# The next chunk's projection moved into the middle of a top-k chunk, ahead of its last two blocks, with one dot per top-k step

## The chip, the cores and the metric

The kernel runs on one core of one Trainium2 chip. The metric is the device time of one execution in microseconds. A core has a matrix engine (TensorE, PE in the profile, with its weight loads PEld), a vector engine (VectorE, DVE), a scalar engine (ScalarE, ACT), GpSimd (POOL), and SyncE (SP), which here only issues DMAs. Each engine works through its own queue in order and waits on semaphores for the others.

## The reference

Two layers over 512 tokens of width 1024. Each has a mixer (pooling and retention in layer 0, a gated recurrence in layer 1) and then PEER, a channel mixer that picks experts by product keys. The change touches PEER only, and it is the same in both layers:

```python
q = (xt @ w_q).reshape(T, PEER_HEADS, 2, PEER_HALF)
s = jnp.einsum('thpd,hpkd->thpk', q, sub_keys)
s_top, i_top = lax.top_k(s, PEER_TOPK)
cand = s_top[:, :, 0, :, None] + s_top[:, :, 1, None, :]
best, pos = lax.top_k(cand, PEER_TOPK)
eid = ...
gate = jax.nn.softmax(best, axis=-1)
act = jax.nn.gelu(jnp.einsum('td,thkd->thk', xt, u_sel))
return jnp.einsum('thk,thkd->td', gate * act, v_sel)
```

There are 8 heads with two halves each, 128 keys per half, the best 16 of each, and 16 experts of 16384 per token and head.

## The kernel before, in words

Weights come from DRAM by `stream` (L172): SP loads 512 KB into one of five `raw` buffers, ScalarE casts it to a rounded part `hi` (L169), and VectorE takes the rest as `lo` (L170). There are six `hi`/`lo` buffers. TensorE then multiplies in three passes (`mm3`, L185 to L187). A buffer is free again when TensorE has used it.

Most of PEER is done densely. For all 16384 experts the activation of tokens 32 to 383 is computed in 128 blocks of 128 experts (`mm1`, 24 matmuls of 352 columns each); the result is multiplied with a gate array that holds zeros nearly everywhere, and multiplied with the v table (`mm2`, L1098). 84 of the 128 blocks (`lookahead`, L756) can be done before the gates are known: they are the work that fills TensorE while VectorE does the routing. They are called lookahead blocks below.

`route_topk` (L767) does the routing in four chunks of two heads (four half-heads). In each chunk TensorE makes the q projection (`proj_T`, 4 x 24 matmuls of 512 columns; ScalarE copies each of the four heads to `qh`, L781), then for each of four token blocks (tb 0 to 3, 128 tokens each) four score matmuls (L851). VectorE finds the top 16 of each half-head in five steps (L860 to L864; one such group is called a head below), twenty steps per token block.

Token block 0 is finished chunk by chunk: `choose` picks the experts of two heads, and `Scatter.place` (L78) computes their addresses. The first 32 tokens of block 0 are not done densely: for them GpSimd fetches the u rows of their experts by indirect DMA (`urow`, L741, eight fetches of 128 rows per chunk, into seven buffers), VectorE takes eight dots per chunk (L105), and `weigh` (L107) puts a Gelu of the dots on ScalarE (`actu`, L111) and multiplies it into the gates (L113). Then `Scatter.add` (L116) adds the gates of block 0 into the DRAM array `gz`, sixteen indirect DMAs per head on GpSimd (L127). Each head's adds wait for those of the head before. On GpSimd's queue stand: chunk 0's rows, the adds of head 0, chunk 1's rows, the adds of head 1, chunk 2's rows, the adds of head 2, chunk 3's rows, and all other adds.

After the chunks, token blocks 3, 1 and 2 get their `choose` for all eight heads, `route_gates` (L885) builds the gate array (VectorE makes one-hot tiles, TensorE multiplies them, L912 and L913, ScalarE scales, SP stores to `gd`, L918), and `experts` (L998) reads `gd` and `gz` back and runs the expert matmuls.

How much lookahead stands between the routing steps is set by credits that the generators yield:

```python
for cost in gen:
    credit += cost
    while credit >= 2.8:
        credit -= 2.8
        next(look, None)
```

A yield of 2.8 thus emits one lookahead block. The order of instructions within an engine is then set by a scheduler that follows the emitted order with its own estimate of times; `tc.issue_after` holds an instruction behind another one.

Before the change, a chunk emits: projection; for each token block its scores, its four heads, and a yield of 1.5 to 4 (`YC`, by chunk); after block 0 `choose`, and after blocks 2 and 3 four dots each. The four weight tiles of the next projection are streamed ahead of the last four dots.

Of the kernel before, what the change touches and what calls it, by code (L numbers as in the profile page):

```python
# [9 lines left out]
F32 = mybir.dt.float32  # L10
F32R = mybir.dt.float32r
F16 = mybir.dt.float16
U32 = mybir.dt.uint32
# [7 lines left out]
P = 128  # L21
T = 512
NTB = T // P
D = 1024
# [12 lines left out]
QC = 32 // QN  # L37
# [7 lines left out]
RAW = 5  # L45
QS = 8
Y2 = 1.6
YC = (1.5, 3.0, 3.0, 4.0)
AHEAD = 4
TAIL = 4  # L50
CREDIT0 = 0.0
# [2 lines left out]
NEG = -3.0e38  # L54
# [88 lines left out]
class Kern:  # L143
# [589 lines left out]
        return xT  # L733

    def urow(self, pool, layer, ids, j):
        if self.urows % 7 == 6:
            t = self.pe.tile([P, D], F32, name="urow3", tag="lnb")
        else:
            t = pool.tile([P, D], F32, name="urow", tag="urow", bufs=6)
        self.urows += 1  # L740
        d = self.nc.gpsimd.indirect_dma_start(out=t, out_offset=None, in_=self.io["u%d" % layer],  # L741
                                              in_offset=bass.IndirectOffsetOnAxis(ap=ids[:, j:j + 1], axis=0))
        return t, d.ins
# [23 lines left out]
    def route_topk(self, layer, xT, kT, gz):  # L767
        nc, tc, io = self.nc, self.tc, self.io
        with tc.tile_pool(name="rt", bufs=1) as rt, tc.tile_pool(name="rt2", bufs=2) as rt2, \
# [5 lines left out]
            stop = rt.tile([P, NTB, 16, 16], F32, name="stop", tag="stop")  # L775
            itop = rt.tile([P, NTB, 16, 16], F16, name="itop", tag="itop")
            wq = io["peer_w_q"][layer]

            def sink_q(n, ps):
                q = rt2.tile([P, T], F32, name="qh", tag="qh", bufs=5)  # L780
                nc.scalar.copy(q, ps)  # L781
                qs.append(q)

# [55 lines left out]
                nc.scalar.copy(ghT, gs)  # L839
                nc.vector.tensor_tensor(glT, gs, ghT, ALU.subtract)  # L840

            for c in range(4):
                qs = []
                keys = rt2.tile([P, 4, P], F32, name="keys", tag="keys")
                nc.sync.dma_start(out=keys, in_=io["keysT"][layer][:, c * 4:c * 4 + 4, :])
                self.proj_T(wq, c, xT, sink_q, early=c == 0)
                for tb in range(NTB):
                    ts = slice(tb * P, (tb + 1) * P)
                    ps = self.psB.tile([P, 512], F32, name="pB", tag="pB")
                    for i in range(4):  # L850
                        nc.tensor.matmul(ps[:, i * P:(i + 1) * P], qs[i][:, ts], keys[:, i, :],  # L851
                                         start=True, stop=True)
                    ixs = rs2.tile([P, 4, 16], U32, name="ix", tag="ix", bufs=2)
                    for i in range(4):
                        hp = c * 4 + i
                        sc = ps[:, i * P:(i + 1) * P]
                        mx = stop[:, tb, hp, :]
                        ix = ixs[:, i, :]
                        s2 = rs2.tile([P, P], F32, name="s2", tag="s2")
                        nc.vector.max(out=mx[:, 0:8], in_=sc)  # L860
                        nc.vector.max_index(out=ix[:, 0:8], in_max=mx[:, 0:8], in_values=sc)
                        nc.vector.match_replace(out=s2, in_to_replace=mx[:, 0:8], in_values=sc, imm_value=NEG)
                        nc.vector.max(out=mx[:, 8:16], in_=s2)
                        top = nc.vector.max_index(out=ix[:, 8:16], in_max=mx[:, 8:16], in_values=s2)  # L864
                    nc.vector.tensor_copy(itop[:, tb, c * 4:c * 4 + 4, :], ixs)
                    yield YC[c]
                    if tb == 0:
                        yield from choose(0, c * 2, 2)
                        if c:
                            gz.add(self)  # L870
                    else:
                        n = (0, 1, 1)[tb - 1] * QC // 2
                        if tb == 3 and c < 3:
                            self.w0 = [self.stream(wq[c + 1, k]) for k in range(4)]
                        yield 1.3 * n
                        with tc.issue_after(top.ins):
                            gz.dots(self, n)
                gz.weigh(self, rs2)
                if c == 0:
                    gz.add(self)  # L880
# [350 lines left out]
```

## Time and profile before

| what | value |
|---|---|
| median of three runs | 2781.21 us (2779.95 to 2781.95) |
| the profiled execution | 2778.95 us |
| its span | 2777.2 us |
| TensorE busy | 2737.9 us (99%) |
| VectorE busy | 2357.1 us (85%) |
| first score of layer 0, of layer 1 | 188.9 us, 1624.2 us |
| last scores of layer 0, of layer 1 | 412.0 us, 1847.6 us |
| gate matmuls of layer 0 | 525.9 to 619.1 us |
| gate matmuls of layer 1 | to 2054.5 us |

Times in the profile count from the start of the span. "Busy" of VectorE is overstated a little in the top-k stages: one instruction's record overlaps the next one's by 0.1 us or so, and what counts is the distance from start to start. The same holds for TensorE, whose matmuls are pipelined: 24 matmuls with records of 0.32 us each take 24 times the step between their starts. A wait in square brackets is the idle time ahead of an instruction, with what ended it.

### The profile page before, as it was taken

To read this page: it belongs to the slowest core of one execution; us is meant where nothing else is said; L and a number is where in the kernel's file an instruction comes from. 1 tells how busy PE (TensorE), PEld (TensorE's weight loads), DVE (VectorE), ACT (ScalarE), POOL (GpSimd) and SP (SyncE) were. 2 spreads that over 40 slices of the span, in tenths; PEclk is the share of its full clock that TensorE was granted. 3 is DMA by queue.
4 is the path that set the end of the run, shared out by engine and by line. 5 is a ranking of instruction groups with operands and counts; after the bars stand their busy time and mean duration, and the time that the engine had idled before them with its cause. 6 is when DMAs were issued, how large, how long until landed. Compare 5 with 4: busy or idle time off the path is not lost.

```text
span 2777.2 us, 41653 instructions
## 1 busy us (share of the span) xinstructions
PE 2737.9 (99%) x15314; PEld 2442.7 (88%) x15314; DVE 2357.1 (85%) x4556; ACT 1115.8 (40%) x1575; POOL 1344.2 (48%) x865
## 2 busy tenths in 40 slices
PE   9999899999999999999999998999999999999998
PEld 7898899999888888888788898999998888888886
DVE  6678789886899989998798678789868999899988
ACT  3353335553333333333334343346553333333332
POOL 0006558774556555653000017558754566566652
PEclk9999999999999999999999999999999999999999
DMA  6357677899999999998222557667999999999994
GB/s 231 122 183 218 205 220 203 225 301 367 355 396 406 394 403 400 404 396 307 96 84 73 205 176 200 196 215 189 266 310 344 396 407 406 386 389 409 404 380 172
DMA packets 319470, 794.12 MB, mean 286 GB/s; under 512 B 62240, under 2 KB 128288, under 8 KB 319264
## 3 DMA queue, kind: packets, MB, share of 16 engines
q1 hardware_dynamic: 176384, 413.64, 42.1%
q0 software_dynamic: 120128, 303.22, 31.0%
q10 hardware_dynamic: 22752, 74.59, 6.7%
q8 instruction: 120, 1.97, 0.3%
q14 instruction: 86, 0.70, 0.1%
HBM read 711.38 MB, written 79.95 MB: 285 GB/s over the span
## 4 chain that ended last, share of the span: by engine, by line
PE 85%; issue 7%; DVE 3%; POOL 3%; DMA 2%; ACT 0%; SPq 0%; DVEq 0%; POOLq 0%; ACTq 0%
PE pC L1098 19%; PE pB L1098 19%; PE pA L187 11%; PE pA L185 11%; PE pA L186 11%; PE pC L185 3%; PE pC L187 3%; PE pC L186 3%; POOL gz L127 2%; DMA urow<-in_u,ids 1%; PE pB L912 1%; PE pB L913 1%; PE pB L851 1%; DVE oh L902 1%; POOL urow L741 1%
## 5 line engine op out<-in xcount | busy, mean ns | idle before, releaser
L169 ACT CAST hi<-raw 128x1024 fp32r<-128x1024 f32 (+1 forms) x609 | 636.3, 1050 | 920.3 <-PE pC L1098 216.0
L170 DVE TENSOR_TENSOR lo<-raw,hi 128x1024 fp32r<-128x1024 f32 (+1 forms) x609 | 730.3, 1215 | 188.6 <-ACT hi L169 183.2
L970 POOL DMA_INDIRECT row<-in_u,eid x256 | 402.6, 1573 | 441.7 <-DVE av L982 392.5
L185 PE MATMUL pA<-xThi,hi 128*128 128x352 f32 (+2 forms) x1808 | 606.7, 336 | 1.9 <-ACT hi L169 1.4
L187 PE MATMUL pA<-xThi,lo 128*128 128x352 f32 (+2 forms) x1808 | 604.3, 334 | 0.9 <-DVE lo L170 0.9
L186 PE MATMUL pA<-xTlo,hi 128*128 128x352 f32 (+2 forms) x1808 | 604.1, 334 | 0.8 <-DVE xTlo L170 0.8
L127 POOL DMA_INDIRECT gz<-gate,idx x256 | 494.2, 1930 | 132.4 <-issue 79.9
L970 POOL DMA_INDIRECT row<-in_v,eid x256 | 356.2, 1391 | 145.0 <-DVE h L995 66.8
L995 DVE SCALAR_TENSOR_TENSOR h<-row,cf,h 128x1024 f32<-128x1024 f32 x256 | 329.6, 1288 | 42.7 <-DMA row<-in_v,eid 42.0
L185 PEld LDWEIGHTS pA<-xThi,hi 128*128 128x128 f32 x1808 | 339.7, 188 | 19.2 <-ACT hi L169 2.5
L186 PEld LDWEIGHTS pA<-xTlo,hi 128*128 128x128 f32 x1808 | 339.6, 188 | 16.7 <-DVE xTlo L170 1.2
L187 PEld LDWEIGHTS pA<-xThi,lo 128*128 128x128 f32 x1808 | 339.5, 188 | 16.5 <-DVE lo L170 2.2
L982 DVE CUSTOM_DVE_ANT_0 row<-row,x 128x1024 f32<-128x1024 f32 x256 | 311.3, 1220 | 20.7 <-DMA row<-in_u,eid 20.4
L1098 PE MATMUL pC<-hi,ch 128*128 128x512 f32 x768 | 299.1, 389 | 0.0
L1098 PE MATMUL pB<-hi,cl 128*128 128x512 f32 x768 | 299.1, 389 | 0.0
L1098 PE MATMUL pB<-hi,ch 128*128 128x512 f32 x768 | 299.0, 389 | 0.0
L1098 PE MATMUL pC<-lo,ch 128*128 128x512 f32 x768 | 299.0, 389 | 0.0
L1098 PE MATMUL pC<-hi,cl 128*128 128x512 f32 x768 | 298.9, 389 | 0.0
L1098 PE MATMUL pB<-lo,ch 128*128 128x512 f32 x768 | 298.8, 389 | 0.0
L187 PE MATMUL pC<-xThi,lo 128*128 128x352 f32 x672 | 218.6, 325 | 17.4 <-DVE lo L170 17.3
L169 ACT CAST ch<-gt 128x768 fp32r<-128x768 f32 x128 | 107.1, 837 | 311.1 <-DVE gt L1061 216.8
L185 PE MATMUL pC<-xThi,hi 128*128 128x352 f32 x672 | 220.4, 328 | 0.1
(280 smaller groups left out, 4410.5 us busy)
## 6 DMA issues: line engine op xcount, KB each, us to landing
raw<-in_peer_ut SPq DMA_DIRECT2D x256, 512.0 KB, 6.6
raw<-in_peer_v SPq DMA_DIRECT2D x256, 512.0 KB, 7.6
gd<-gbuf SPq DMA_DIRECT2D x16, 2048.0 KB, 10.5
gt<-gd ACTq DMA_DIRECT2D x60, 512.0 KB, 7.6
sp<-ge SPq DMA_DIRECT2D x38, 704.0 KB, 5.1
ge<-sp ACTq DMA_DIRECT2D x38, 704.0 KB, 8.3
raw<-in_peer_w_q SPq DMA_DIRECT2D x32, 512.0 KB, 4.8
gz<-zero SPq DMA_DIRECT2D x64, 256.0 KB, 4.2
```

What stands on the lines that cost most here:

```text
L127: d = nc.gpsimd.indirect_dma_start(out=flat, out_offset=bass.IndirectOffsetOnAxis(ap=self.idx[c][:, j:j + 1], axis=0), in_=gate[:, j:j + 1 ...
L169: self.nc.scalar.copy(hi, src)
L170: return self.nc.vector.tensor_tensor(lo, src, hi.bitcast(F32), ALU.subtract)
L185: nc.tensor.matmul(ps, ah, bh, start=(first and i == 0), stop=False)
L186: nc.tensor.matmul(ps, ah, bl, start=False, stop=False)
L187: nc.tensor.matmul(ps, al, bh, start=False, stop=(last and i == n - 1))
L741: d = self.nc.gpsimd.indirect_dma_start(out=t, out_offset=None, in_=self.io["u%d" % layer], in_offset=bass.IndirectOffsetOnAxis(ap=ids[:, ...
L851: nc.tensor.matmul(ps[:, i * P:(i + 1) * P], qs[i][:, ts], keys[:, i, :], start=True, stop=True)
L970: nc.gpsimd.indirect_dma_start(out=t, out_offset=None, in_=io[name], in_offset=bass.IndirectOffsetOnAxis(ap=at, axis=0))
L982: dot = nc.vector.tensor_tensor_reduce(ur, ur, x, 1.0, 0.0, ALU.mult, ALU.add, av[:, k:k + 1])
L995: nc.vector.scalar_tensor_tensor(acc, vr, c, acc, ALU.mult, ALU.add)
L1098: nc.tensor.matmul(acc[hf], a[:, ts], b[:, hf * 512:(hf + 1) * 512], start=first and i == 0, stop=last and i == 2)
```

## The change

A chunk is now emitted in another order. The projection of chunk 0 comes first. Then, in each chunk: scores and heads of token block 0, with a yield of `YA` = 2.3 after each head; `choose`; scores and heads of block 1, each head with one of the four weight tiles of the next projection and a yield of 2.3; the scores of blocks 2 and 3 together; the whole next projection; and then the eight heads of blocks 2 and 3, each followed by one dot (held behind the head's last step) and a yield of `YB`, 0.2 in chunks 0 to 2 and 2.4 in chunk 3. `keys` has one buffer instead of two, `qh` four instead of five, and `urow` eight buffers in all instead of seven.

```diff
-YC = (1.5, 3.0, 3.0, 4.0)
+YA = 2.3
+YB = (0.2, 0.2, 0.2, 2.4)
...
-        if self.urows % 7 == 6:
+        if self.urows % 8 == 7:
             t = self.pe.tile([P, D], F32, name="urow3", tag="lnb")
         else:
-            t = pool.tile([P, D], F32, name="urow", tag="urow", bufs=6)
+            t = pool.tile([P, D], F32, name="urow", tag="urow", bufs=7)
...
-                q = rt2.tile([P, T], F32, name="qh", tag="qh", bufs=5)
+                q = rt2.tile([P, T], F32, name="qh", tag="qh", bufs=4)
...
-            for c in range(4):
-                qs = []
-                keys = rt2.tile([P, 4, P], F32, name="keys", tag="keys")
...
-                self.proj_T(wq, c, xT, sink_q, early=c == 0)
-                for tb in range(NTB):
...
-                    yield YC[c]
-                    if tb == 0:
-                        yield from choose(0, c * 2, 2)
-                        if c:
-                            gz.add(self)
-                    else:
-                        n = (0, 1, 1)[tb - 1] * QC // 2
-                        if tb == 3 and c < 3:
-                            self.w0 = [self.stream(wq[c + 1, k]) for k in range(4)]
-                        yield 1.3 * n
-                        with tc.issue_after(top.ins):
-                            gz.dots(self, n)
+            qs, w0 = [], []
+            keys = project(0)
+            for c in range(4):
+                for _ in top16(c, 0, scores(0)):
+                    yield YA
+                yield from choose(0, c * 2, 2)
+                if c:
+                    gz.add(self)
+                for i, _ in enumerate(top16(c, 1, scores(1))):
+                    if c < 3:
+                        w0.append(self.stream(wq[c + 1, i]))
+                    yield YA
+                late = [scores(tb) for tb in (2, 3)]
+                if c < 3:
+                    self.w0, w0 = w0, []
+                    keys = project(c + 1)
+                for tb in (2, 3):
+                    for top in top16(c, tb, late[tb - 2]):
+                        with tc.issue_after(top):
+                            gz.dots(self, QC // 8)
+                        yield YB[c]
                 gz.weigh(self, rs2)
```

`scores`, `project` and `top16` are the old statements put into functions: `project` loads `keys` (one buffer) and calls `proj_T`; `top16` yields after each head.

On TensorE, the projection for chunk 1, where it begins and some rows further on. Before (128x512 are its matmuls, 128x352 those of lookahead blocks):

```order
L185 MATMUL pC<-xThi,hi 128x352
L186 MATMUL pC<-xTlo,hi 128x352
L185 MATMUL pA<-xThi,hi 128x352
L186 MATMUL pA<-xTlo,hi 128x352
L185 MATMUL pA<-xThi,hi 128x512
L186 MATMUL pA<-xTlo,hi 128x512
L187 MATMUL pA<-xThi,lo 128x512
...
L185 MATMUL pA<-xThi,hi 128x512
L186 MATMUL pA<-xTlo,hi 128x512
L187 MATMUL pC<-xThi,lo 128x352
L185 MATMUL pC<-xThi,hi 128x352
```

After (its first row is the end of a lookahead block):

```order
L188 MATMUL pC<-xThi,lo 128x352
L846 MATMUL pB<-keys,qh 128x128 x8
L186 MATMUL pA<-xThi,hi 128x512
L187 MATMUL pA<-xTlo,hi 128x512
L188 MATMUL pA<-xThi,lo 128x512
L186 MATMUL pA<-xThi,hi 128x512
```

Before, two lookahead blocks were begun, broken off where their `lo` was not expected yet, and finished between the projection's matmuls, and the scores of block 3 stood ahead of all that (28 lookahead matmuls earlier). Now the scores of blocks 2 and 3 stand together, and all 96 matmuls of the projection follow without a lookahead block among them.

On VectorE, the first dots of chunk 1 (`urow` is the fetched row, `xx` the tokens). Before:

```order
L861 MAX_INDEX ix<-stop,pB 128x8
L864 MAX_INDEX ix<-stop,s_2640 128x8
L105 ISA urow,avu<-urow,xx 128x1024
L105 ISA avu 128x1
L865 CAST itop<-ix 128x64
L105 ISA urow,avu<-urow,xx 128x1024
L105 ISA avu 128x1
L105 ISA urow,avu<-urow,xx 128x1024
L105 ISA avu 128x1
L105 ISA urow,avu<-urow,xx 128x1024
L105 ISA avu 128x1
L862 MATCH_REPLACE s_2723<-stop,pB 128x128
```

After:

```order
L171 TENSOR_TENSOR lo<-raw,hi 128x1024 x2
L865 MAX stop<-pB 128x8 x2
L866 MAX_INDEX ix<-stop,pB 128x8
L867 MATCH_REPLACE s_2924<-stop,pB 128x128
L865 MAX stop<-pB 128x8
L868 MAX stop<-s_2924 128x8
L866 MAX_INDEX ix<-stop,pB 128x8
L869 MAX_INDEX ix<-stop,s_2924 128x8
L106 ISA urow,avu<-urow,xx 128x1024
L106 ISA avu 128x1
L867 MATCH_REPLACE s_2931<-stop,pB 128x128
```

Four dots in a row became one dot behind each head; the two `lo` of the next lookahead blocks now stand ahead of the first head of block 2, and none between there and the last dot.

On ScalarE, the copies of the four projected heads (`qh`) around the Gelu of chunk 1's dots (`actu`), with the casts of streamed tiles (`hi`). Before:

```order
L781 COPY qh<-pA 128x512
L111 ACTIVATE actu<-avu 32x8 x4
L781 COPY qh<-pA 128x512 x2
L169 CAST hi<-raw 128x1024 x4
L781 COPY qh<-pA 128x512
```

After:

```order
L782 COPY qh<-pA 128x512 x3
L170 CAST hi<-raw 128x1024 x2
L112 ACTIVATE actu<-avu 32x8 x4
L170 CAST hi<-raw 128x1024 x2
L782 COPY qh<-pA 128x512
```

The Gelu moved from behind the first copy to ahead of the last one, with two casts between it and that copy.

More of the change, by code (lines that the diff above doesn't have):

```diff
@@ L840, in choose, with scores @@
                 nc.vector.tensor_tensor(glT, gs, ghT, ALU.subtract)
-            for c in range(4):
-                qs = []
-                keys = rt2.tile([P, 4, P], F32, name="keys", tag="keys")
+            def scores(tb):
+                ps = self.psB.tile([P, 512], F32, name="pB", tag="pB")
+                for i in range(4):
+                    nc.tensor.matmul(ps[:, i * P:(i + 1) * P], qs[i][:, tb * P:(tb + 1) * P], keys[:, i, :],
+                                     start=True, stop=True)
+                return ps
@@ L845, in route_topk, with project @@
+            def project(c):
+                qs.clear()
+                keys = rt2.tile([P, 4, P], F32, name="keys", tag="keys", bufs=1)
                 nc.sync.dma_start(out=keys, in_=io["keysT"][layer][:, c * 4:c * 4 + 4, :])
                 self.proj_T(wq, c, xT, sink_q, early=c == 0)
-                for tb in range(NTB):
[L848 to L865, printed above, removed]
-                    yield YC[c]
-                    if tb == 0:
-                        yield from choose(0, c * 2, 2)
-                        if c:
-                            gz.add(self)
-                    else:
-                        n = (0, 1, 1)[tb - 1] * QC // 2
-                        if tb == 3 and c < 3:
-                            self.w0 = [self.stream(wq[c + 1, k]) for k in range(4)]
-                        yield 1.3 * n
-                        with tc.issue_after(top.ins):
-                            gz.dots(self, n)
@@ new lines, in project, with top16 @@
+                return keys
+            def top16(c, tb, ps):
+                ixs = rs2.tile([P, 4, 16], U32, name="ix", tag="ix", bufs=2)
+                for i in range(4):
+                    hp = c * 4 + i
+                    sc = ps[:, i * P:(i + 1) * P]
+                    mx = stop[:, tb, hp, :]
+                    ix = ixs[:, i, :]
+                    s2 = rs2.tile([P, P], F32, name="s2", tag="s2")
+                    nc.vector.max(out=mx[:, 0:8], in_=sc)
+                    nc.vector.max_index(out=ix[:, 0:8], in_max=mx[:, 0:8], in_values=sc)
+                    nc.vector.match_replace(out=s2, in_to_replace=mx[:, 0:8], in_values=sc, imm_value=NEG)
+                    nc.vector.max(out=mx[:, 8:16], in_=s2)
+                    yield nc.vector.max_index(out=ix[:, 8:16], in_max=mx[:, 8:16], in_values=s2).ins
+                nc.vector.tensor_copy(itop[:, tb, c * 4:c * 4 + 4, :], ixs)
```

## The prediction

> **What bounds the kernel now.** I read the page first, then the busy time by stage, then TensorE's waits, then the instructions around its two long ones.
>
> ```profile
> PE 2737.9 (99%) x15314; PEld 2442.7 (88%) x15314; DVE 2357.1 (85%) x4556; ACT 1115.8 (40%) x1575; POOL 1344.2 (48%) x865
> ```
> ```profile
> 186.00:300.00 114.00, 104.95 (x603) 97.33 (x602) 99.32 (x426) 47.02 (x74) 63.18 (x41) 0.96 0.67 209
> ...
> 352.00:415.00 63.00, 62.57 (x362) 58.30 (x361) 51.66 (x212) 26.11 (x41) 36.26 (x24) 1.00 0.67 201
> 415.00:520.00 105.00, 105.00 (x667) 104.95 (x667) 95.58 (x355) 58.49 (x77) 85.15 (x43) 1.00 0.76 217
> ...
> 1620.00:1740.00 120.00, 109.50 (x634) 101.09 (x634) 99.21 (x426) 47.73 (x75) 68.96 (x43) 0.97 0.68 204
> ```
>
> After each stretch stand its length, the busy time of PE, PEld, DVE, ACT and POOL, and the granted clock. TensorE sets the time. The change reorders work and keeps its amount, so it can win only what TensorE loses in the two top-k stages: 9.05 us idle in the first row, 0.43 in the second, 10.5 in layer 1. In the third row (the last chunk's end and the large choices) nothing is lost.
>
> ```profile
> PE pC L187 <- DVE lo L170: 17.3, 5, 8.9
> ```
> ```profile
> 289.91 0.66 PE L187 MATMUL pC<-xThi,lo 128*128 128x352 f32 x1 [7.39 <-DVE lo L170]
> 290.37 0.49 PE L185 MATMUL pC<-xThi,hi 128*128 128x352 f32 x1
> 290.66 0.49 PE L186 MATMUL pC<-xTlo,hi 128*128 128x352 f32 x1
> ...
> 1726.62 0.66 PE L187 MATMUL pC<-xThi,lo 128*128 128x352 f32 x1 [8.87 <-DVE lo L170]
> ...
> 1729.13 0.49 PE L186 MATMUL pC<-xTlo,hi 128*128 128x352 f32 x1
> ```
> ```profile
> 284.00:286.00 2.00, 0.00 (x0) 0.00 (x0) 2.00 (x8) 0.00 (x0) 1.70 (x2) 0.92 1.01 412
> 294.00:296.00 2.00, 2.00 (x9) 2.00 (x8) 2.00 (x6) 0.00 (x0) 1.72 (x1) 0.52 0.70 207
> ```
> ```profile
> 236.66 0.17 DVE L113 TENSOR_TENSOR gate<-gate,actu 32x32 f32<-32x32 f32 x1
> ...
> 277.12 1.22 DVE L105 CUSTOM_DVE_ANT_0 urow<-urow,xx 128x1024 f32<-128x1024 f32 x1 [2.92 <-DMA urow<-in_u,ids]
> ...
> 283.98 1.22 DVE L105 CUSTOM_DVE_ANT_0 urow<-urow,xx 128x1024 f32<-128x1024 f32 x1 [0.82 <-DMA urow<-in_u,ids]
> 286.33 1.21 DVE L170 TENSOR_TENSOR lo<-raw,hi 128x1024 fp32r<-128x1024 f32 x1
> ```
> ```profile
> 237.12 1.61 POOL L127 DMA_INDIRECT gz<-gate,idx  x1 [14.18 <-DVE gate L113]
> ...
> 267.98 1.27 POOL L741 DMA_INDIRECT urow<-in_u,ids  x1 [0.30 <-issue]
> ```
>
> So one wait stands in each layer, in the second chunk. Weighing chunk 0 (236.66) starts sixteen scatter-adds on GpSimd; chunk 1's u rows queue behind them until 267.98, and the first lands at 277.12. VectorE stands in front of four dots, and the `lo` that TensorE needs comes after them. TensorE loses 7.39 + 8.87 = 16.3 us, and more behind it: the clock falls about 3.2 us into the wait (0.92 in the first slice) and stays at half to about 295.9, so that steps take 0.293 us (290.37 to 290.66). From 289.91 that costs 6.0 x (1 - 0.158/0.293) = 2.8 us, in layer 1 2.8 us of slow running, 1.3 (0.158 is the normal step, below). Together 20.4. The other idle time is 1.7 + 0.4 + 1.6 = 3.7, short waits in chunk 0 above all. At stake: 24.1 us.
>
> **The change, part by part.**
>
> ```profile
> 193.77 0.32 PE L185 MATMUL pC<-xThi,hi 128*128 128x352 f32 x1
> 197.57 0.61 PE L851 MATMUL pB<-keys,qh 128*128 128x128 f32 x4
> ...
> 206.97 1.05 PE L851 MATMUL pB<-keys,qh 128*128 128x128 f32 x8
> ```
> ```profile
> 230.41 0.39 PE L186 MATMUL pA<-xTlo,hi 128*128 128x512 f32 x1
> ...
> 244.27 0.40 PE L187 MATMUL pA<-xThi,lo 128*128 128x512 f32 x1
> ```
>
> A lookahead block (24 matmuls) takes 197.57 - 193.77 = 3.80 us. From 197.57 to 206.97 stand eight scores and two blocks: 1.8 for eight scores. A projection is 96 steps of (244.27 - 230.41)/61 = 0.227: 21.8.
>
> *Dots under the projection.* VectorE's late phase is now eight heads and eight dots alternately, while TensorE runs a projection whose weights are all split.
>
> ```profile
> 219.78 1.20 DVE L105 CUSTOM_DVE_ANT_0 urow<-urow,xx 128x1024 f32<-128x1024 f32 x1
> ...
> 220.93 1.21 DVE L105 CUSTOM_DVE_ANT_0 urow<-urow,xx 128x1024 f32<-128x1024 f32 x1
> ...
> 225.10 1.21 DVE L170 TENSOR_TENSOR lo<-raw,hi 128x1024 fp32r<-128x1024 f32 x1
> ...
> 227.41 1.21 DVE L170 TENSOR_TENSOR lo<-raw,hi 128x1024 fp32r<-128x1024 f32 x1
> ```
>
> A dot takes 1.15 (219.78 to 220.93), a `lo` with a head 2.31, so a head 1.2. The phase: 8 x 1.15 + 8 x 1.2 + 0.9 (estimate, for the first head, whose steps have nothing to overlap) = 19.7 us, against 21.8 of cover. It removes both long waits: where TensorE stood waiting for a `lo`, it now multiplies by weights split long ago. What is late next stands on ScalarE.
>
> *The last q copy.* ScalarE now has the Gelu of the dots and two `hi` casts ahead of the copy of the fourth q head, and the next scores need that copy. The Gelu waits for the last dot.
>
> ```profile
> 235.65 0.86 ACT L111 ACTIVATE actu<-avu 32x8 f32<-32x8 f32 x4 [1.24 <-DVE avu L105]
> 240.38 1.05 ACT L169 CAST hi<-raw 128x1024 fp32r<-128x1024 f32 x1 [0.55 <-PE pA L186]
> 245.42 0.58 ACT L781 COPY qh<-pA 128x512 f32<-128x512 f32 x1
> ```
>
> From the last dot to the copy's end: 0.1 + 0.86 + 2 x 1.05 + 0.6 = 3.7 us. In layer 0, on the clock of the trace: four blocks now precede the second scores, so 197.57 + 7.6 = 205.2, scores 0.9, four blocks, 221.3; eight scores, 223.1; projection, 244.9. VectorE's last `lo` ahead of the phase needs the buffer of the block that ends at 221.3: 1.05 for `hi`, 1.15 for `lo`, 223.5, dots done at 243.2, copy at 246.9. TensorE wants it after three scores and five matmuls, at 246.3: 0.6 us of wait in each layer.
>
> *Second chunk.* From 246.9: 18.2 of blocks, 0.9, three blocks, 1.8, projection, one block, three scores (0.7): TensorE wants the copy at 305.7. Weighing now comes at 243.2 + 1.2 = 244.4, not 236.66.
>
> ```profile
> 1671.93 0.17 DVE L113 TENSOR_TENSOR gate<-gate,actu 32x32 f32<-32x32 f32 x1
> ...
> 1714.08 1.23 DVE L105 CUSTOM_DVE_ANT_0 urow<-urow,xx 128x1024 f32<-128x1024 f32 x1 [4.63 <-DMA urow<-in_u,ids]
> 1716.60 1.23 DVE L105 CUSTOM_DVE_ANT_0 urow<-urow,xx 128x1024 f32<-128x1024 f32 x1 [1.18 <-DMA urow<-in_u,ids]
> ```
>
> From weighing to the first row landed are 40.5 us in layer 0 and 42.2 in layer 1, so the first dot starts at 284.9 (layer 1: 1.7 later); VectorE would be ready at 281.8. Rows land 2.3 to 2.5 us apart (277.12 to 283.98 in three steps; 1714.08 to 1716.60), a head and a dot take 2.35: with 2.45, dots end at 284.9 + 7 x 2.45 + 1.15 = 303.2, the copy at 306.9. Wait: 1.2 us, in layer 1 2.9. Bounds: nothing, if rows land 1.2 earlier; 5 us, if they come 2 later. I take 1.2 and 2.9.
>
> *Third and fourth chunk.* POOL is free before the rows are asked for, so VectorE's phase starts with the scores: the copy stands 2.2 + 19.7 + 3.7 = 25.6 after the last block, wanted after 1.8 + 21.8 + 3.8 + 0.7 = 28.1. No wait. In the last chunk no projection covers the phase, but six split blocks (six buffers) do, 22.8 us, and one more `lo` stands inside it. No wait.
>
> *First chunk.* Four weight splits come early, 4 x 1.15 on VectorE ahead of the eighth block; I leave 0.5 us per layer of the short waits there. Single `keys` and fewer q buffers: the `keys` load waits for scores which TensorE has done when it starts the projection, and has 21.8 us to land. The loads queued behind it on SP have five raw buffers ahead of them. Nothing. The seventh urow buffer lets all eight rows be asked for at once: GpSimd's queue no longer waits for a dot.
>
> *Start of the experts.* Of the blocks between the last gate matmul and the first expert matmul, six are left of nine; three were used earlier.
>
> ```profile
> 619.09 0.22 PE L913 MATMUL pC<-og,oh 128*128 128x128 f16 x1
> ...
> 653.41 0.40 PE L1098 MATMUL pB<-hi,ch 128*128 128x512 f32 x1
> ```
> ```profile
> 631.34 1.21 POOL L138 DMA_DIRECT2D gt<-gz  x2 [12.89 <-DMA raw<-in_peer_v]
> ```
> ```profile
> DMA to landing us min/median/max: 8.7/9.1/9.6
> ```
>
> The read of `gz` is issued 12.0 us after the last gate matmul ends (619.3) and lands 8.7 to 9.6 later; product and cast take some 1.8. That is 22.5 to 23.4 against 22.8 of blocks: 0.3 us per layer, at most 2 if a split stands in front.
>
> *Sum.* 24.1 - (0.5 + 0.6 + 1.2 + 0.3) - (0.5 + 0.6 + 2.9 + 0.3) = 17.2 us won. The profiled execution took 2778.95 (span 2777.2 and 1.75 around it): 2761.7. The median of the runs, 2781.21, lies 2.3 above it, so **2764.0**.
>
> *A rule weighed.* Waits under about 3.2 us left the clock whole in the rows above, and my 2.9 in layer 1 is near that. The Trainium skill, "TensorE: Matmul & The Clock Gate", Part 1 (the clock gate), says that TensorE falls to half rate after an idle window of about 3.4 us, a window that runs freely. By it the sum stays, or rises by one slow stretch in a run whose window falls badly; the trace agrees with half rate and with about 3 us, but ran slow for 6.0 us after the wait in layer 0 and 2.8 in layer 1, where the page has one window.
>
> **Rivals.**
>
> *All of it.* The rows land in time, no wait for the copy in chunk 1: 24.1 - 2.8 = 21.3 won, 2760. For it: GpSimd's sixteen adds do not depend on the rest. Chance 0.2.
>
> *Late rows.* If chunk 1's rows come 2.6 us later (adds ran 2 us longer in layer 1 already), the waits are 3.8 and 5.5 and the clock falls in both: 5.2 + 2.8 + 1.3 = 9.3 less, 8 won, 2773. Chance 0.18.
>
> *Dots outlast the projection (slower).* If the phase takes 26 us instead of 19.7, because dots and heads stretch beside GpSimd's adds, the copy is late at every boundary: 6.9, 6.1 and 3.8 in layer 0, 1.7 more in layer 1; 35 us, some 12 of half rate over six waits, and 1.6: 49 against 24, so 25 slower, 2806. It decides from 23.4 us on: two boundaries in two layers cost 4 us for each, past 2.5 all three cost 6. Against it: dots and heads ran at 1.15 and 1.2. Chance 0.09.
>
> *Experts late.* The full 2 us of each layer, 3 lost more: 2767. Chance 0.1.
>
> **How the numbers follow.** The forecast has 0.43. Range 2756 to 2778: a little under "all of it", for short waits that go too, and beyond late rows. A change under 0.2% (5.6 us) can't be told from none. Faster (under 2775.6): forecast, all of it, experts, and a third of late rows, 0.79; same 0.12; slower 0.09.
>
> **What would show it.** Right: no TensorE wait for a `lo` over 3 us in the top-k stages; chunk 1's first dot still waiting for its row by some 3 us; a TensorE wait of 1 to 3 us for `qh` at the third chunk's first scores; first weighing about 8 us later. Wrong: a clock at 0.5 in these stages, a `qh` wait at all boundaries, or a wait of several us at the first expert matmul.

## The result, and the profile after

The changed kernel takes 2761.51 us, the median of six runs (2758.41 to 2764.77), against 2781.22 for the kernel before in the same comparison (2776.03 to 2782.49). The ratio is 0.993, with a 95% interval of 0.9919 to 0.994: 19.7 us won, between 17 and 23. The profiled execution is the slowest of the six, 2764.77 (span 2763.0), so it shows 14.2 us of the gain. The other 5.5 lie between the profiled executions and the medians, 2.3 on the side of before and 3.3 on this one.

The span cut at four places that both kernels have (TensorE's first score and first expert matmul in each layer) shows where the 14.2 us are:

| stretch | before | after | won |
|---|---|---|---|
| start to first score, layer 0 | 188.87 | 189.68 | -0.8 |
| routing, layer 0 (to the first expert matmul) | 464.54 | 452.85 | 11.7 |
| experts of layer 0 and the mixer of layer 1 | 970.74 | 972.86 | -2.1 |
| routing, layer 1 | 464.70 | 455.86 | 8.8 |
| experts of layer 1, to the end | 688.35 | 691.75 | -3.4 |

Routing won 20.5 us. 5.5 were given back behind it, where the experts start. TensorE's waits of the changed kernel (total, times, longest):

```profile
PE pB L846 <- ACT qh L782: 3.4, 2, 2.2
PE pB L1113 <- ACT ch L170: 3.3, 2, 1.7
```

The 17.3 us of `pC` waiting for `lo` are gone. In their place stand two for the copied q head and two for `ch`, the experts' operand. The stages (length, busy time of PE, PEld, DVE, ACT, POOL, granted clock):

```profile
186.00:300.00 114.00, 114.00 (x666) 106.27 (x665) 98.82 (x411) 48.93 (x74) 56.85 (x37) 1.00 0.68 215
300.00:352.00 52.00, 50.84 (x302) 48.59 (x301) 47.45 (x190) 20.88 (x36) 41.62 (x26) 1.00 0.81 245
352.00:415.00 63.00, 63.00 (x387) 60.97 (x386) 55.67 (x227) 27.91 (x44) 43.30 (x26) 1.00 0.70 215
...
1620.00:1740.00 120.00, 117.75 (x667) 109.74 (x667) 106.25 (x442) 48.59 (x77) 69.46 (x42) 0.99 0.69 213
```

The first row idled 9.05 us before and nothing now, and its clock is whole. In layer 1, 10.5 us of idle time became 2.25. What happens in chunk 1 now, on VectorE (the first dots and the last), ScalarE and TensorE:

```profile
284.56 1.23 DVE L106 CUSTOM_DVE_ANT_0 urow<-urow,xx 128x1024 f32<-128x1024 f32 x1 [2.23 <-DMA urow<-in_u,ids]
289.01 1.23 DVE L106 CUSTOM_DVE_ANT_0 urow<-urow,xx 128x1024 f32<-128x1024 f32 x1 [2.02 <-DMA urow<-in_u,ids]
...
302.84 1.21 DVE L106 CUSTOM_DVE_ANT_0 urow<-urow,xx 128x1024 f32<-128x1024 f32 x1
```
```profile
304.09 0.86 ACT L112 ACTIVATE actu<-avu 32x8 f32<-32x8 f32 x4 [4.08 <-DVE avu L106]
...
306.88 0.57 ACT L782 COPY qh<-pA 128x512 f32<-128x512 f32 x1
```
```profile
305.52 0.83 PE L846 MATMUL pB<-keys,qh 128*128 128x128 f32 x6
...
307.51 0.49 PE L846 MATMUL pB<-keys,qh 128*128 128x128 f32 x2 [1.16 <-ACT qh L782]
```

VectorE still stands before late rows (2.23 and 2.02 us), but nothing that TensorE needs stands behind those dots except the Gelu, and behind the Gelu the copy. The 7.39 us became 1.16.

### The profile page after: what moved, and what is told of

Read it like the earlier page. It is cut to its first block, busy times and chain, and to the rows that moved or that the text cites. A ratio compares the mean times of both kernels' runs of the same rounds, so it can differ in the third digit from the quotient of the medians.

```text
span 2763.0 us, 41651 instructions
## 1 busy us (share of the span) xinstructions
PE 2735.9 (99%) x15314; PEld 2445.2 (88%) x15314; DVE 2368.5 (86%) x4556; ACT 1112.3 (40%) x1575; POOL 1345.3 (49%) x865
## 4 chain that ended last, share of the span: by engine, by line
PE 91%; DVE 3%; DMA 2%; POOL 1%; issue 1%; ACT 1%; SPq 0%; DVEq 0%; POOLq 0%; ACTq 0%
PE pB L1113 18%; PE pC L1113 18%; PE pA L186 12%; PE pA L188 12%; PE pA L187 12%; PE pC L186 4%; PE pC L187 4%; PE pC L188 4%; POOL gz L128 1%; DMA row<-in_u,eid 1%; PE pB L846 1%; PE pB L927 1%; DMA gd<-gbuf 1%; PE pB L928 1%; DVE urow L106 1%
## 5 line engine op out<-in xcount | busy, mean ns | idle before, releaser
L985 POOL DMA_INDIRECT row<-in_u,eid x256 | 394.6, 1541 | 434.2 <-DVE av L997 388.4
L128 POOL DMA_INDIRECT gz<-gate,idx x256 | 511.9, 1999 | 154.9 <-issue 76.9
L187 PEld LDWEIGHTS pA<-xTlo,hi 128*128 128x128 f32 x1808 | 339.6, 188 | 16.3 <-DVE xTlo L171 0.7
```

Of the source, the lines that this page charges most:

```text
L128: d = nc.gpsimd.indirect_dma_start(out=flat, out_offset=bass.IndirectOffsetOnAxis(ap=self.idx[c][:, j:j + 1], axis=0), in_=gate[:, j:j + 1 ...
L187: nc.tensor.matmul(ps, ah, bl, start=False, stop=False)
L985: nc.gpsimd.indirect_dma_start(out=t, out_offset=None, in_=io[name], in_offset=bass.IndirectOffsetOnAxis(ap=at, axis=0))
```

## The experiments

The theory on trial is the prediction's: TensorE's loss was a `lo` queued on VectorE behind dots whose rows came late, the projection now covers those dots, and what is left is the Gelu ahead of the last q copy and the experts' start. The rivals: only the rows' lateness matters, only the spacing of the dots matters, or the credits (fewer blocks behind the gates, more ahead of the late phase) do it. Medians of one kernel on several chips differ a little, so the ratio to the kernel before in the same comparison counts.

| kernel | median us | ratio to before, 95% | routing 0 / 1, profiled | experts 0 / 1, profiled |
|---|---|---|---|---|
| the change | 2761.5 | 0.9919 to 0.994 | 452.9 / 455.9 | 972.9 / 691.8 |
| b_no_first_adds | 2768.4 | 0.9942 to 0.9971 | 463.0 / 455.2 | 970.9 / 687.9 |
| b_spread_dots | 2821.7 | 1.0133 to 1.0162 | 488.5 / 482.9 | 970.6 / 687.9 |
| a_four_dots | 2768.7 | 0.9945 to 0.9971 | 454.9 / 456.7 | 977.4 / 688.9 |
| a_more_dots | 2781.7 | 0.9993 to 1.0011 | 464.2 / 462.7 | 972.7 / 689.0 |
| a_blocks_late | 2754.6 | 0.9889 to 0.9918 | 453.2 / 452.7 | 970.8 / 687.9 |
| a_nine_left | 2774.4 | 0.9969 to 0.999 | 466.0 / 458.5 | 970.7 / 687.9 |
| a_gelu_late | 2760.9 | 0.9911 to 0.9938 | 451.7 / 455.7 | 974.5 / 689.0 |
| a_rows_later | 2760.8 | 0.9909 to 0.9937 | 451.6 / 452.8 | 971.0 / 689.2 |
| a_both | 2765.1 | 0.9921 to 0.9949 | 455.1 / 453.1 | 973.0 / 689.3 |
| a_seven_rows | 2758.4 | 0.9896 to 0.9926 | 451.9 / 453.7 | 972.1 / 690.8 |
| a_no_first_adds | 2776.0 | 0.9977 to 0.9995 | 461.5 / 457.1 | 972.7 / 689.6 |
| a_rows_held | 2778.2 | 0.9985 to 1.0002 | 463.2 / 461.9 | 972.1 / 692.1 |

### Rows, spacing and cover: what makes the gain

**b_no_first_adds** is the kernel before, with this edit at the end of `route_topk`:

```diff
                 if c == 0:
-                    gz.add(self)
+                    gz.todo.pop(0)
```

> The kernel before, with the sixteen scatter-adds of head 0 left out in both layers (their gates never reach gz); nothing else is changed. Late rows (my theory): what TensorE lost in the second chunk came from u rows that queue behind these adds, so the first dot of chunk 1 finds its row landed, the two lo waits of 7.39 and 8.87 us and the half clock behind them (4.1 us) go, and the time falls by about 20 to 2761 (2757 to 2766), as far as with the change itself. Rival, the order of work: four dots in a row ahead of a lo hold TensorE whether the rows are there or not, and only the change of order cures that; then a lo wait of 3 us or more stays in each layer and the time stays above 2770.

12.4 us won of the 20 expected, between the two expectations. TensorE's long waits in layer 0 and in layer 1, and VectorE's dots ahead of the first:

```profile
287.64 0.66 PE L187 MATMUL pC<-xThi,lo 128*128 128x352 f32 x1 [4.31 <-DVE lo L170]
...
1717.48 0.43 PE L187 MATMUL pC<-xThi,lo 128*128 128x352 f32 x1 [1.48 <-DVE lo L170]
```
```profile
279.06 1.23 DVE L105 CUSTOM_DVE_ANT_0 urow<-urow,xx 128x1024 f32<-128x1024 f32 x1 [1.72 <-DMA urow<-in_u,ids]
...
281.71 1.23 DVE L105 CUSTOM_DVE_ANT_0 urow<-urow,xx 128x1024 f32<-128x1024 f32 x1 [1.42 <-DMA urow<-in_u,ids]
```

The adds were a large part of the cause, not all of it. In layer 0 the rows are asked for from 264.8 on, when their numbers are ready. That is only 3.2 us earlier than before (267.98), and the third and fourth row still come 1.72 and 1.42 us late; TensorE's wait fell from 7.39 to 4.31. In layer 1 the same four dots waited 0.34 us for rows in all, and TensorE's wait fell from 8.87 to 1.48. So with rows nearly in time the order of work still cost 1.48 us there. In layer 0 this run does not part lateness from order, since the rows stayed late.

**b_spread_dots** is the kernel before, with a dot behind each head of blocks 2 and 3 in place of the two groups of four, and the next weight tiles streamed ahead of block 3's heads:

```diff
                         top = nc.vector.max_index(out=ix[:, 8:16], in_max=mx[:, 8:16], in_values=s2)
+                        if tb > 1:
+                            yield 1.3
+                            with tc.issue_after(top.ins):
+                                gz.dots(self, 1)
```

> The kernel before with one part of the change alone: one dot behind each head of token blocks 2 and 3 instead of four in a row behind the fourth; projection, buffers and credits stay, the four weight tiles are streamed ahead of block 3's heads. My theory: the place of the projection does most of it, so the lo waits stay: lo splits still stand behind dots whose rows are late, 4 us or more in chunk 1 of each layer, and the time is 2772 to 2780. Rival, spacing does it: waits under 3 us, 2768 or less.

41.7 us slower than before, beyond both expectations. TensorE's wait in chunk 0 (17.56 us in layer 1), and VectorE in it:

```profile
229.30 0.66 PE L187 MATMUL pA<-xThi,lo 128*128 128x352 f32 x1 [18.30 <-DVE lo L170]
```
```profile
217.59 1.23 DVE L105 CUSTOM_DVE_ANT_0 urow<-urow,xx 128x1024 f32<-128x1024 f32 x1 [1.37 <-DMA urow<-in_u,ids]
222.31 1.23 DVE L105 CUSTOM_DVE_ANT_0 urow<-urow,xx 128x1024 f32<-128x1024 f32 x1 [3.01 <-DMA urow<-in_u,ids]
...
226.53 1.21 DVE L105 CUSTOM_DVE_ANT_0 urow<-urow,xx 128x1024 f32<-128x1024 f32 x1
228.03 1.22 DVE L170 TENSOR_TENSOR lo<-raw,hi 128x1024 fp32r<-128x1024 f32 x1
229.83 1.21 DVE L105 CUSTOM_DVE_ANT_0 urow<-urow,xx 128x1024 f32<-128x1024 f32 x1
```

Here the `lo` of the next lookahead block is sorted in between the spread dots, behind four of them, and two of these come early enough to wait 1.37 and 3.01 us for their rows. TensorE, without a projection to run, waits 18.3 us. Without those 4.4 us some 14 would be left (an estimate), so lateness is the smaller part here, and a spread phase without cover was worse than four dots in a row. Since the weight tiles moved too, the 41.7 us are not the price of spacing alone, but this shows that spacing by itself is not the gain.

**a_four_dots.**

```diff
                     for top in top16(c, tb, late[tb - 2]):
-                        with tc.issue_after(top):
-                            gz.dots(self, QC // 8)
                         yield YB[c]
+                    with tc.issue_after(top):
+                        gz.dots(self, QC // 2)
```

> The changed kernel, but with the dots four at a time behind the fourth head of token blocks 2 and 3, as they stood before, and the projection still ahead of both. My theory: it is the projection over pre-split weights that covers the dots, not their spacing; in chunk 1 rows land 2.3 to 2.5 us apart and dots end within 1 us of where they end now (304.0 in layer 0), so the time is the same within 2: 2761.5 (2759 to 2764). Rival, one dot per step is what does it: dots in a row stand before late rows with the heads queued behind them, the last dot comes 3 us or more later, and each such us is TensorE's in both layers: 2768 or more.

7.2 us slower than the change, as the rival had it in size but not in place. In chunk 1 the last dot of layer 0 starts at 301.94 instead of 302.84, as I expected. The time goes elsewhere, at the fourth chunk's first scores (2.18 us in layer 1 as well) and at the experts' start:

```profile
369.69 0.49 PE L846 MATMUL pB<-keys,qh 128*128 128x128 f32 x2 [1.98 <-ACT qh L782]
```
```profile
655.92 0.79 PE L1113 MATMUL pB<-hi,ch 128*128 128x512 f32 x1 [3.65 <-ACT ch L170]
```

Most of the gain is there with dots in fours (12 of 20 us), so the projection's new place, with the credits that go with it, carries it, and the spacing adds the rest. In the profiled execution the largest single loss is 4.5 us at the experts' start of layer 0. No run moves the projection alone in the kernel before: that its place is what counts rests on this run, b_spread_dots and a_blocks_late together.

**a_more_dots.**

```diff
             k.nc.vector.tensor_tensor_reduce(r, r, k.xx, 1.0, 0.0, ALU.mult, ALU.add, self.av[:, j:j + 1])
+            if twice:
+                k.nc.vector.tensor_tensor_reduce(r, r, k.xx, 1.0, 0.0, ALU.mult, ALU.add, self.spare[:, j:j + 1])
...
-                            gz.dots(self, QC // 8)
+                            gz.dots(self, QC // 8, tb == 2)
```

> The changed kernel with four more dots in each chunk: behind each head of token block 2 the dot is done a second time into a spare column, 4 x 1.15 = 4.6 us more of VectorE in each late phase, nothing else added (the order then puts the Gelu behind the last q copy and two lo ahead of the last dots). It tells how much room the projection leaves. My theory, as in the sum on record: a phase of 19.7 us has room for 3.7 more (it decides from 23.4 on); with 24.3 the late end of VectorE reaches TensorE at every boundary, as a wait for qh or for a lo of 3 to 6 us in chunks 0 and 1 and of 1 to 3 in chunk 2, some with half clock behind: 20 to 35 us slower than the changed kernel, 2781 to 2797. Rival: only the chunk with late rows is on TensorE's path and there the dots wait for rows anyway, so little changes: 2768 or less.

20 us slower than the change, at the lower end of the theory's range, but not at the places it named. No wait of 0.4 us stands at the first two boundaries; TensorE runs dry in the middle of chunk 2 (layer 1 has the same waits, and both layers one of 1.9 us in the last chunk):

```profile
333.30 0.43 PE L191 MATMUL pC<-xThi,lo 128*128 128x352 f32 x1 [1.28 <-DVE lo L174]
337.90 0.43 PE L189 MATMUL pA<-xThi,hi 128*128 128x352 f32 x1 [0.84 <-ACT hi L173]
341.86 0.66 PE L191 MATMUL pA<-xThi,lo 128*128 128x352 f32 x1 [3.37 <-DVE lo L174]
```

In this kernel's order the Gelu stands behind the copy, so VectorE's lateness no longer meets TensorE at the boundary. It is carried on through the next chunk until the split blocks are used up. I read this as follows: the cover is not one projection against one phase, but VectorE's total over a chunk against TensorE's. No run tests that reading by itself.

### The credits, and the experts' start

**a_blocks_late.**

```diff
-YA = 2.3
-YB = (0.2, 0.2, 0.2, 2.4)
+YA = 1.2
+YB = (1.3, 1.3, 1.3, 2.4)
```

> The changed kernel with the credits moved within a chunk: YA 1.2 instead of 2.3 and YB 1.3 instead of 0.2 in chunks 0 to 2, so that three to four lookahead blocks of a chunk, with their lo splits, move from ahead of the projection to behind it, among the dots; and nine blocks instead of six stand between the last gate matmul and the first expert matmul. My theory: the q copy is no longer wanted right behind the projection, so its wait goes, but lo splits stand behind dots again and in chunk 1 a lo wait of 1 to 4 us comes in its place in each layer; at the experts' start the waits of 1.6 and 1.7 us go: in all 2755 to 2764. Rival, the blocks must stand ahead of the phase: a lo wait of over 5 us comes back in chunk 1 of both layers, and the time is above 2768.

The best kernel: 2754.61, 6.9 us below the change, with a ratio interval that just doesn't touch the change's, and a little under the range that I expected. In the routing it has only short waits, the longest 1.14 us, and they stand in chunk 2, not in chunk 1:

```profile
322.47 0.43 PE L186 MATMUL pC<-xThi,hi 128*128 128x352 f32 x1 [0.53 <-ACT hi L170]
328.74 0.43 PE L188 MATMUL pC<-xThi,lo 128*128 128x352 f32 x1 [1.14 <-DVE lo L171]
```

It leaves nine blocks behind the gates, as the kernel before did, and puts fewer ahead of the late phase than the change, and it wins more. So the change's choice of credits is not what makes the gain.

**a_nine_left.**

```diff
-YB = (0.2, 0.2, 0.2, 2.4)
+YB = (0.2, 0.2, 0.2, 1.3)
```

> The changed kernel with YB of the last chunk at 1.3 instead of 2.4, so that nine lookahead blocks instead of six stand between the last gate matmul and the first expert matmul; chunks 0 to 2 as they are. It tells what moving blocks late gained at the experts' start and what within the chunks. My theory: the ch waits (1.58 and 1.67 us, with 1.5 of half clock) go, 4.5 us: 2757 (2755 to 2759), and the qh waits stay; the rest of what the kernel with late blocks won (2754.6) is theirs. Rival: the last chunk misses these blocks, lo waits of 2 us or more come up there, and the time is 2761 or more.

The stretches behind the routing are back at the length of before (970.7 and 687.9), as the theory said. But the time rose by 13 us, as the rival said: the last chunk misses the blocks, and a second loss, with waits for which the profile names no cause but issue, came up at chunk 2's sixteen scores in a row:

```profile
343.24 0.50 PE L846 MATMUL pB<-keys,qh 128*128 128x128 f32 x3 [1.50 <-issue]
344.72 0.41 PE L846 MATMUL pB<-keys,qh 128*128 128x128 f32 x2 [0.98 <-issue]
```
```profile
438.19 0.66 PE L188 MATMUL pC<-xThi,lo 128*128 128x352 f32 x1 [4.06 <-DVE lo L171]
```

Of the two ways tried to leave nine blocks for the experts' start, only that of a_blocks_late was free. It takes the three blocks from the front of the last chunk, and moves others within chunks 0 to 2.

**a_rows_later.**

```diff
-            done, used = 0, 0.0
+            done, used = 0, -2.0
```

> The changed kernel, with the first two dots of the experts' gather of token block 3 put off by one pair of expert blocks (the count of used cost starts at -2 instead of 0). My theory: TensorE's waits for ch at the second pair (1.58 us in layer 0, 1.67 in layer 1 with 1.5 of half clock behind it) come from the product of gates standing behind four row dots on VectorE whose rows have not landed; with two of them moved on, the product is ready earlier and the waits shrink to 0.5 or less: 2757 (2755 to 2760). Rival: the read of gz or the v table's splits set the second pair, and nothing changes: 2761.5 within 1.5; or the rows put off come back at the end of the experts: 2763.

In the changed kernel TensorE waits at the second pair of expert blocks, and VectorE does four row dots ahead of the product `gt` which that pair needs:

```profile
646.19 1.23 DVE L997 CUSTOM_DVE_ANT_0 row<-row,x 128x1024 f32<-128x1024 f32 x1 [3.00 <-DMA row<-in_u,eid]
...
649.52 1.23 DVE L997 CUSTOM_DVE_ANT_0 row<-row,x 128x1024 f32<-128x1024 f32 x1
650.67 0.08 DVE L997 DVE_READ_ACCUMULATOR2_ANT av<- 128x1 f32 x1
650.67 0.89 DVE L1076 TENSOR_TENSOR gt<-gt,ge 128x704 f32<-128x704 f32 x1
```
```profile
652.48 0.50 PE L1113 MATMUL pB<-hi,ch 128*128 128x512 f32 x1 [1.58 <-ACT ch L170]
```

With two of these dots put off, the product starts 6.1 us after the first expert matmul (640.29) instead of 8.1 (642.53), and no wait of 0.5 us is left there:

```profile
646.39 0.89 DVE L1076 TENSOR_TENSOR gt<-gt,ge 128x704 f32<-128x704 f32 x1
```

So the mechanism is as the theory has it, and the profiled execution took 2754.99. The other four took 2760.2 to 2762.4, and the median is the change's within a microsecond. Its trace has no half rate in the stages at all, not even behind a `qh` wait of 2.17 us, and that is in part chance (see the last section). What the unprofiled executions lose instead isn't seen, so this stays unsettled as a gain.

**a_gelu_late** and **a_both**.

```diff
-        for q in range(QN):
-            nc.scalar.activation(act[:NU, q * QC:(q + 1) * QC], self.av[q * NU:(q + 1) * NU], AF.Gelu)
+        with k.tc.issue_after(k.qcopy.ins):
+            for q in range(QN):
+                nc.scalar.activation(act[:NU, q * QC:(q + 1) * QC], self.av[q * NU:(q + 1) * NU], AF.Gelu)
```

Here `qcopy` is the last copy to `qh`. a_both has this edit and that of a_rows_later.

> The changed kernel, with the Gelu of a chunk's dots held behind the copy of the last projected q head on ScalarE. My theory: the wait for qh in chunk 1 is nothing but the Gelu standing ahead of that copy, so the copy no longer depends on the dots and the waits of 1.16 and 2.25 us and some 1.7 of half clock go: 2756.5 (2754 to 2759). The price is that weighing of chunk 0 comes about 4 us later (behind four lo), so chunk 1's rows land 4 us later too, which nothing on TensorE's path sees. Rival: those later rows put the dots ahead of lo splits that TensorE wants next, and a lo wait takes the place of the qh wait: 2761 or more.

> Both of the last two edits together. My theory: the two waits lie in different stages, so the gains add up: 5 and 4.5, 2752 (2749 to 2756), and the longest TensorE waits left in the routing and at the experts' start are under 1 us. Rival: VectorE is so full in these stages that what one edit frees the other takes: 2757 or more.

The waits for `qh` are gone, and waits for `lo` took their place in chunk 2, as the rival said (1.17 us in layer 0; this one in layer 1):

```profile
1762.75 0.43 PE L189 MATMUL pA<-xThi,lo 128*128 128x352 f32 x1 [2.72 <-DVE lo L172]
```

In a_both they are 3.00 and 3.09 us, and the gains did not add up: 2765.1 instead of 2752. The time is the change's within the interval, in both kernels. The Gelu only decided where TensorE met VectorE's lateness; a_more_dots points the same way.

**a_seven_rows.**

```diff
-        if self.urows % 8 == 7:
+        if self.urows % 7 == 6:
...
-            t = pool.tile([P, D], F32, name="urow", tag="urow", bufs=7)
+            t = pool.tile([P, D], F32, name="urow", tag="urow", bufs=6)
```

> The changed kernel with seven urow buffers in all, as before, instead of eight. My theory: the eighth buffer plays no part; the last row of a chunk is asked for after the first dot, still lands before its own dot 16 us later, and the time is the same within 1.5: 2761.5. Rival: GpSimd's queue stands before that row until the first dot of the chunk, in chunk 1 the adds of head 1 behind it start 6 us or more later and the rows of chunk 2 with them, so a qh wait of 2 us or more comes up in chunk 2 and the time is 2766 or more.

The median is 3.2 us below the change's, more than the 1.5 that I allowed, and the two ratio intervals overlap. So no loss shows, and the gain does not need the eighth buffer; whether seven are a little better is not settled.

### Rows that come early

**a_no_first_adds** has the edit of b_no_first_adds on the changed kernel.

> The changed kernel, with the sixteen scatter-adds of head 0 left out in both layers. Late rows (my theory): what is left of the wait in chunk 1 (1.16 us for qh in layer 0, 2.25 in layer 1, and about 1.7 of half clock behind the second) has the same cause and goes: 5 us, 2756.5 (2754 to 2759), and the first dot of chunk 1 doesn't wait for its row. Rival, ScalarE's order: the copy is late because the Gelu of the last dot and two casts stand ahead of it, rows or no rows; then a qh wait of at least 1 us stays in each layer and the time falls by less than 2.

Wrong by both: 14.5 us slower than the change, though the waits for `qh` in chunk 1 did go. TensorE lost its time at the sixteen scores in a row of chunk 1 (in layer 0 of chunk 2 too), with waits put down to nothing but issue:

```profile
277.56 0.60 PE L846 MATMUL pB<-keys,qh 128*128 128x128 f32 x4
278.98 0.73 PE L846 MATMUL pB<-keys,qh 128*128 128x128 f32 x5 [0.82 <-issue]
280.43 0.47 PE L846 MATMUL pB<-keys,qh 128*128 128x128 f32 x2 [0.72 <-issue]
...
281.85 0.61 PE L846 MATMUL pB<-keys,qh 128*128 128x128 f32 x4 [0.44 <-issue]
```

From the first start to the last they take 4.6 us; in the changed kernel 1.7. The three groups together cost 9.9 us more than there, and the 3.4 or 3.5 us at half rate behind each of them 4.8. Less the 5.0 that the `qh` waits had cost, that is 9.7, and the profiled execution's routing is 9.9 longer than the change's. In the microseconds of the first group (276 to 284) u rows land, in the queue of GpSimd's DMAs (packets, MB, share of the engines' time), here and in the changed kernel:

```profile
q0 software_dynamic: 970, 2.56, 83.4%
```
```profile
q0 software_dynamic: 430, 0.52, 34.9%
```

**a_rows_held** was to tell whether these transfers are the cause. It is a_no_first_adds, with chunk 1's eight row requests moved from `place` into a function `ask`:

```diff
                 late = [scores(tb) for tb in (2, 3)]
+                if c == 1:
+                    with tc.issue_after(self.scored.ins):
+                        gz.ask(self, rs2)
+                    gz.add(self)
```

> The changed kernel without the sixteen adds of head 0, as before, and with chunk 1's eight rows asked for only behind the scores of token block 3 in that chunk. It tells why rows that came early cost time: with them, the sixteen scores of blocks 2 and 3 in chunk 1 took from 277.56 to 282.46 instead of 1.95 us, with 2.2 us of waits put down to issue, at a DMA share of 1.02 to 1.09. Theory: TensorE gets these short matmuls late because the rows' transfers fill the DMA engines; held rows leave the sixteen scores of chunk 1 at 1.95 us without a wait in both layers, those of chunk 2, where nothing is held, keep theirs, and the time falls from 2776 by 3 to 6, since rows asked for at 280 bring back a qh wait of 1 to 2 us. Rival: the stalls have another source in this order of instructions; then the waits of 2.2 and 2.1 us stay in chunk 1 although no row is on its way.

It told nothing on that. The hold only ordered the instructions and made no engine wait: the rows were asked for from 268.08 to 277.08 as without it, ahead of scores at 279.83, and from the first start to the last the scores took 5.0 us. Two of the waits (0.80 and 0.79 us) came on lookahead matmuls just ahead of the scores. The cause of these stalls stays open.

## Why the prediction was right, and where its steps failed

**The long waits** (16.3 us, and 4.1 of half clock behind them) went, by the mechanism given: the dots now stand under multiplications whose weights are split. Its times for layer 0 came within 0.8 us: dots of chunk 0 done at 243.5 (243.2), chunk 1's first dot at 284.6 (284.9), its last dot done at 304.0 (303.2), the copy done at 307.5 (306.9).

**The q copy.** No wait for chunk 0's (0.6 forecast in each layer), 1.16 and 2.25 us for chunk 1's (1.2 and 2.9; the parts of the sum for TensorE come to 305.5, not 305.7, which makes it 1.4), none in the third and fourth chunk. The 0.5 for chunk 0's short waits didn't show either. With nothing of these lost, routing won a little more than forecast: 20.5 us in the profiled execution, against 24.1 - 2.3 - 4.0 = 17.8.

**The experts' start** is the term that was mis-sized: 0.3 us per layer, at most 2, against 2.1 and 3.4 in the profiled execution. I looked at the first pair of expert blocks, which had no wait, and at the read of `gz`. The wait is one pair later: VectorE's four row dots of the gather stand ahead of the second pair's product, and their rows are still on the way (one came 3.00 us late), since the three blocks that gave them time are gone: in both kernels with nine blocks left the stretch is as long as before.

**The clock.** "Waits under about 3.2 us left the clock whole" failed. Two waits of 2.25 and 1.67 us were followed by 3.5 and 3.4 us at half rate, about 1.6 us of loss each. The first of these lies in a top-k stage and is one of the prediction's own signs of being wrong, a clock at 0.5. The trace of before already had a counterexample, in the mixer of layer 1 (the second row's 0.50 is the granted clock):

```profile
1338.42 1.38 PE L252 MATMUL pC<-c_ident,h 128*128 128x128 f32 x8 [2.17 <-DVE h L288]
```
```profile
1340.40:1343.80 3.40, 3.40 (x9) 2.62 (x10) 3.40 (x7) 0.03 (x1) 0.00 (x0) 0.50 0.47 154
```

The Trainium skill's rule, "TensorE: Matmul & The Clock Gate", Part 1, was weighed with the words that the sum stays or rises by one slow stretch where the free-running window falls badly. The profiled execution shows two such stretches, behind waits shorter than the window of about 3.4 us that the rule has.

**Cover.** The prediction has 23.4 us as the length of the phase from which the change is no faster than before, with the loss at the boundaries. In a_more_dots the phase is 4.6 us longer, 24.3 by that sum, and the time is that of before (ratio 0.9993 to 1.0011). So the size was about right and the place was not: the loss came in the middle of chunk 2. That kernel has another order on ScalarE, so the agreement in size may be chance. And the first adds were not all of the lateness: without them b_no_first_adds won 12.4 of 20.

The forecast of 2764.0 lies 2.5 us above the median, and part of that closeness is chance. For a profiled execution it said 2761.7, 3.1 too low. There the experts' start with the half clock behind its wait cost 4.9 us more than forecast and the mixer ahead of the routing 0.8, and routing won 2.7 more: errors of both signs. The medians then lie 5.5 us further apart than the two profiled executions.

## What to carry to other kernels

Ask of each slow, uncertain instruction what stands behind it on its engine, and move the waiting to where that queue holds nothing that the bounding engine needs within the wait's length; making the wait itself shorter won less here. When a cover is taken from one place (three lookahead blocks), look at the next consumers behind it, not only at the first. And two repairs that each remove a wait in the profile may still win nothing, because the late engine meets the bounding one a little further on.

## What the hardware showed that was not expected

**Half clock after short waits.** The same wait of 2.25 us was followed by half rate in the changed kernel and by full rate in a_nine_left (a step is 0.158 us at full rate and 0.293 at half):

```profile
1734.30 0.49 PE L846 MATMUL pB<-keys,qh 128*128 128x128 f32 x2 [2.25 <-ACT qh L782]
...
1735.10 0.50 PE L188 MATMUL pC<-xThi,lo 128*128 128x352 f32 x1
1735.40 0.50 PE L186 MATMUL pC<-xThi,hi 128*128 128x352 f32 x1
```
```profile
1745.62 0.49 PE L846 MATMUL pB<-keys,qh 128*128 128x128 f32 x2 [2.25 <-ACT qh L782]
...
1746.26 0.32 PE L188 MATMUL pC<-xThi,lo 128*128 128x352 f32 x1
1746.42 0.32 PE L186 MATMUL pC<-xThi,hi 128*128 128x352 f32 x1
```

In the routing and at the experts' start of all these kernels, every wait of 3.37 us or more was followed by half rate. Of those between 1.6 and 3.1 us eight were and eight were not. What decides, as far as these traces show, is where the wait falls. Thirteen of the fourteen traces have half rate outside their ends (a_rows_later has none). In each of them its starts and ends lie on one grid of 3.413 us, to within 0.002 us, and its stretches last one to six steps of that grid; the 10.2 and 6.8 us of the kernel before are three and two. On this grid the changed kernel's wait lies whole in one interval (1731.33 to 1734.74), and half rate begins at that interval's end. The wait of a_nine_left is cut in two at 1744.42, and neither part was enough.

I added up, for each interval at full rate from 150 to 2700 us, the time that TensorE lost in it, from start to start beyond the usual step. All 32 intervals that lost 2.13 us or more were followed by half rate, six of the nine between 1.95 and 2.13, and none that lost less. So about 2 us lost within one interval of 3.41 were enough, in one wait or in several. The Trainium skill's page, "TensorE: Matmul & The Clock Gate", Part 1, has a free-running window of this length, which these traces bear out. It has an idle window of about 3.4 us as the condition, and that is more than they needed.

**Matmuls held up beside GpSimd's transfers.** From the first start to the last, sixteen 128x128 scores in a row took 1.7 to 2.0 us in 79 of the 88 such groups in the change and its ten variants, 2.5 us in one, and 4.6 to 5.4 us in eight (four in a_rows_held, three in a_no_first_adds, one in a_nine_left). In the eight, TensorE went on in bursts that begin 0.7 or 1.4 us apart, to within 0.1 us. In a_rows_held such waits began on lookahead matmuls ahead of the scores, so it is not the scores' shape alone.

From 2 us before the first score to 6 us behind it, GpSimd's queue took 74 to 86% of the DMA engines' time in all eight, and at most 65% in the other eighty. That goes with a long run of GpSimd's transfers, but it is not shown to be the cause: undisturbed groups had up to 100% during the scores themselves (a_rows_later, chunk 0 of layer 0). Transfers of instructions, which the trace lists as queues of their own, don't explain it: around the disturbed group of chunk 1 in a_no_first_adds none starts between 272.5 and 296 us.
